# Two strips of columns for each half's 32x32 products in a block inverse, with the copies split by even and odd blocks

## The chip, the cores and the metric

The kernel runs on one core of one Trainium2 chip. The metric is the device time of one execution in microseconds (us), as the median of several runs. The engines are TensorE (PE for its matmuls, PEld for its weight loads), VectorE (DVE), ScalarE (ACT), GpSimd (POOL) and SyncE (SP, which here only issues DMAs). Each has its own queue of instructions and works through it in order; an instruction that waits for another engine waits on a semaphore and holds up what is queued behind it.

## The reference, cut to what matters

The reference is one decoder layer on 512 tokens of width 1024: a norm, one combined input projection, two mixers side by side (native sparse attention and RWKV-7), gates that merge them, an output projection, and a gated MLP with a short convolution. The change lies in the RWKV-7 mixer, whose recurrence over tokens reads:

```python
    def step(state, inp):
        r_t, w_t, k_t, v_t, a_t, b_t = inp
        sa = jnp.einsum('bhij,bhj->bhi', state, a_t)
        state = state * w_t[:, :, None, :] + sa[..., None] * b_t[:, :, None, :] + v_t[..., None] * k_t[:, :, None, :]
        return state, jnp.einsum('bhij,bhj->bhi', state, r_t)
```

There are 8 heads of size 64. The kernel cuts the 512 tokens into 8 chunks of 64 and works a chunk at a time with matrices. Within a chunk, the term `sa` of a token depends on those of the tokens before it, through a strictly triangular 64x64 matrix N. The kernel needs the inverse of I - N, for each chunk and head: 64 matrices in all.

## The kernel before, in words

A 64x64 triangular inverse is put together from 32x32 blocks. With T1 and T2 the inverses of the two diagonal blocks and N21 the block off the diagonal, the remaining block of the inverse is T2 N21 T1. The 64 matrices lie in the tile `AB`, on 128 partitions. Index `g` (0 or 1) names two groups of 32 matrices each: group 0 uses partitions 0 to 63, group 1 partitions 64 to 127. Index `b` names the first or second half of a group's partitions, so `half(g, b)` is a set of 32 partitions: 0 to 31, 32 to 63, 64 to 95 or 96 to 127. `q` counts the 32 matrices ("blocks") of a group.

The steps around the change, in the order of the code:

- Lines 618 to 633: VectorE computes all 128 inverses of the diagonal blocks at once, in the tile `inv`, row by row.
- Lines 729 to 735: VectorE transposes them, two instructions into `Y1` (line 730) and four into `AB` (line 735). `Y1` is a view of the second and third of the four columns of the tile `sg1`.
- `below(q0)`, line 740: for 16 blocks from `q0` on, and for both groups, one 32x32 by 32x32 product N21 T1. Then ScalarE copies the results from PSUM into `Y1`, through the helper of line 123.
- `left(q0)`, line 749: the second product, which multiplies by T2, and ScalarE's copy of the results into `AB`.
- Lines 760 to 774: TensorE's order is written out by hand here: one dense projection, `below(0)`, `below(16)`, and then parts of another projection (`kv_proj(1, 280)`) in turns with `left(0)` and `left(16)`. VectorE and ScalarE are ordered by a scheduler.
- From line 930 on: the sequential part over chunks. Its first pieces on TensorE are `x_own(0)` (line 922), more parts of the projection, and `compress()` (line 786), which compresses keys and values for attention. `compress()` first makes VectorE add position rows into `Rk` (lines 787 to 796), which again is the memory of `sg1`, the part under `Y1` included; its products (line 808) read `Rk` and weights `raw` that SP has loaded.

A float32 matmul appears in the trace as two passes, each with a weight load and a matmul record. The 32x32 products name two places in TensorE's array: the partitions that the operands come from choose a strip of rows, and the partitions of PSUM that the result goes to choose a strip of columns. All products of one group and one function use one strip of rows and one strip of columns: for `below`, group 0 has rows 0 to 31 and columns 32 to 63, group 1 rows 64 to 95 and columns 96 to 127. PSUM is used through `pa()` and `pb()`, two banks each in turn (`ps_a` and `ps_b`, lines 113 to 117); group 0 writes an `a` bank, group 1 a `b` bank.

The names in the profile: `sg` as an input of a 32x32 product is `Y1`; `ps_a<-sg,AB` and `ps_b<-sg,AB` are `below`, `ps_a<-AB,sg` and `ps_b<-AB,sg` are `left`. `sg<-ps_a` and `sg<-ps_b` (32x512) are ScalarE's copies of `below`, `AB<-ps_a` and `AB<-ps_b` those of `left`. `ps_b<-UV,AB` at 180.30 us is `x_own(0)`. `sg<-QK,prm` are the additions into `Rk`, `ps_mm<-raw,sg` the products with it. `ps_mm<-whi,hh`, `<-whi,hl` and `<-wlo,hh` with 280 columns are the projection that runs between the steps. `whi` and `wlo` are the two parts into which a loaded weight `raw` is split, by ScalarE and by VectorE or GpSimd.

Of the kernel before, what the change touches and what calls it, by code (L numbers as in the profile page):

```python
# [80 lines left out]
def hybrid_block(ctx: ExitStack, tc: tile.TileContext, A: dict, out: bass.AP):  # L81
# [28 lines left out]
    def mmb():  # L110
        return bank("mm", 4)

    def pa():
        return bank("a", 2)

    def pb():
        return bank("b", 2)

    def mm(o, l, r, start, stop):
        te.matmul(o, lhsT=l, rhs=r, start=start, stop=stop)  # L120

    def act(o, i, f=AF.Copy, **kw):
        sc.activation(o, i, f, **kw)  # L123
# [493 lines left out]
    ABq = [AB.rearrange("p c a r t -> p (c a) r t")[:, :, g, :] for g in range(2)]  # L617
# [110 lines left out]
    Y1 = sg1[:, 1:3].rearrange("p m s -> p (m s)").rearrange("p (q s) -> p q s", q=32)  # L728
# [8 lines left out]
    def half(g, b):  # L737
        return slice(64 * g + 32 * b, 64 * g + 32 * b + 32)

    def below(q0):  # L740
        ptr = [pa(), pb()]
        for i in range(16):
            for g in range(2):
                mm(ptr[g][half(g, 1), 32 * i:32 * i + 32], ABq[g][half(g, 0), q0 + i, 32:64], Y1[half(g, 0), q0 + i],
                   True, True)
        for g in range(2):
            act(Y1[half(g, 1), q0:q0 + 16].rearrange("p q s -> p (q s)"), ptr[g][half(g, 1)])

    def left(q0):
        ptr = [pa(), pb()]  # L750
        for i in range(16):
            for g in range(2):
                mm(ptr[g][half(g, 0), 32 * i:32 * i + 32], Y1[half(g, 1), q0 + i], ABq[g][half(g, 1), q0 + i, 32:64],
                   True, True)
        for g in range(2):
            act(ABq[g][half(g, 0), q0:q0 + 16, 32:64], ptr[g][half(g, 0)].rearrange("p (q t) -> p q t", t=32))

    fill = kv_proj(1, 280)
    urgent.clear()
    with tc.manual_schedule(engines={mybir.EngineType.PE, mybir.EngineType.Pool}):  # L760
        for m in range(NGA):
            act(siga[m], dense_fm(hh, hl))
        below(0)
        below(16)
        next(fill)
        left(0)
        next(fill)
        left(16)
        next(fill)
        norm_keys(0)  # L770
        rstd(qss.rearrange("p t h -> p (t h)"), DH)
        for t in range(NT):
            nc.gpsimd.tensor_tensor(heads(qn[:, t]), heads(qn[:, t]), qss[:, t, :, None].to_broadcast([128, 8, DH]),
                                    op=ALU.mult)
# [515 lines left out]
    with tc.manual_schedule(engines=KTS):  # L1290
        for t in range(NT):
            qs = slice(128 * t, 128 * t + 128)
            p = mmb()
# [88 lines left out]
```

## Time and profile before

| | |
|---|---|
| median of 3 runs | 843.86 us (843.79 to 844.13) |
| the profiled execution's own time | 844.05 us |
| its span on the core | 842.3 us |
| PE busy | 829.1 us, 98% of the span |
| DVE, ACT, POOL busy | 514.0, 405.9, 52.4 us |
| granted TensorE clock | 1.0 |
| the 256 records of 32x32 products | 168.74 to 178.23 us |

Times in the trace count from the start of the span. A row of the timeline gives the start of a run of equal instructions, the time it covers, the engine, the line, the operation, the output and inputs, the shape and the number of instructions; an idle time before it and its releaser stand in brackets. "32\*32" before a matmul's shape is the number of rows and columns of the array in use. Matmuls are pipelined: the duration of a record is much longer than the distance to the next start, so distances of starts tell the rate. The timeline gives two decimals, so a rate is best read over many starts.

### The profile page before, as it was taken

To read this page: it belongs to the slowest core of one execution; us is meant where nothing else is said; L and a number is where in the kernel's file an instruction comes from. 1 tells how busy PE (TensorE), PEld (TensorE's weight loads), DVE (VectorE), ACT (ScalarE), POOL (GpSimd) and SP (SyncE) were. 2 spreads that over 40 slices of the span, in tenths; PEclk is the share of its full clock that TensorE was granted. 3 is DMA by queue.
4 is the path that set the end of the run, shared out by engine and by line. 5 is a ranking of instruction groups with operands and counts; after the bars stand their busy time and mean duration, and the time that the engine had idled before them with its cause. 6 is when DMAs were issued, how large, how long until landed. Compare 5 with 4: busy or idle time off the path is not lost.

```text
span 842.3 us, 12845 instructions
## 1 busy us (share of the span) xinstructions
PE 829.1 (98%) x5097; PEld 674.3 (80%) x5097; DVE 514.0 (61%) x998; ACT 405.9 (48%) x784; POOL 52.4 (6%) x69
## 2 busy tenths in 40 slices
PE   7999999999999999999999999999999999999998
PEld 6777778887787886777788988888888888888886
DVE  5477779963556678888675576666556666322222
ACT  6766655452545677677344454444444444221210
POOL 6200020140000110111000000000000000000000
PEclk9999999999999999999999999999999999999999
DMA  7432222335461320010167033333333332223421
GB/s 228 115 82 68 75 75 76 92 104 156 126 126 51 88 63 13 22 31 26 51 204 234 0 99 90 90 97 100 100 100 100 96 90 93 98 100 113 138 75 51
DMA packets 109104, 78.73 MB, mean 93 GB/s; under 512 B 3869, under 2 KB 97748, under 8 KB 109044
## 3 DMA queue, kind: packets, MB, share of 16 engines
q1 hardware_dynamic: 106512, 73.51, 30.0%
q0 software_dynamic: 1472, 1.86, 1.0%
q10 hardware_dynamic: 1060, 2.55, 1.0%
q8 instruction: 40, 0.66, 0.3%
q14 instruction: 20, 0.16, 0.1%
HBM read 74.56 MB, written 2.29 MB: 91 GB/s over the span
## 4 chain that ended last, share of the span: by engine, by line
PE 53%; DVE 0%; DVEq 0%; issue 0%
PE ps_mm L120 52%; PE ps_b L203 0%; PE ps_a L203 0%; PE ps_a L120 0%; PE ps_b L1186 0%; PE ps_mm L1186 0%; DVE x L126 0%; DVEq L1378 0%; PE ps_a L1138 0%
## 5 line engine op out<-in xcount | busy, mean ns | idle before, releaser
L296 DVE TENSOR_TENSOR wlo<-raw,whi 128x1024 fp32r<-128x1024 f32 (+1 forms) x111 | 131.5, 1186 | 187.2 <-PE ps_mm L120 158.8
L120 PE MATMUL ps_mm<-hh,whi 128*128 128x512 f32 (+1 forms) x624 | 242.6, 391 | 0.0
L120 PE MATMUL ps_mm<-hl,whi 128*128 128x512 f32 (+1 forms) x624 | 240.4, 387 | 0.0
L123 ACT ACTIVATE whi<-raw 128x1024 fp32r<-128x1024 f32 (+3 forms) x124 | 123.3, 996 | 171.1 <-PE ps_mm L120 143.0
L120 PE MATMUL ps_mm<-hh,wlo 128*128 128x512 f32 (+1 forms) x624 | 151.8, 384 | 0.0
L120 PEld LDWEIGHTS ps_mm<-hh,whi 128*128 128x128 f32 x624 | 117.3, 188 | 26.7 <-issue 1.3
L120 PEld LDWEIGHTS ps_mm<-hl,whi 128*128 128x128 f32 x624 | 117.4, 188 | 23.5 <-issue 1.0
L120 PEld LDWEIGHTS ps_mm<-hh,wlo 128*128 128x128 f32 x624 | 115.1, 188 | 23.4
L120 PE MATMUL ps_mm<-whi,aT 128*128 128x512 f32 x352 | 84.5, 390 | 0.0
L120 PEld LDWEIGHTS ps_mm<-whi,aT 128*128 128x128 f32 x352 | 65.9, 188 | 14.3 <-issue 0.4
L135 DVE SCALAR_TENSOR_TENSOR cgv<-ps_mm,cw,cgv 128x511 f32<-128x511 f32 (+1 forms) x88 | 65.4, 746 | 1.6
L123 ACT ACTIVATE cgv<-ps_mm,cw 128x512 f32<-128x512 f32 x44 | 34.3, 781 | 23.3 <-PE ps_mm L120 23.3
L120 PE MATMUL ps_mm<-wlo,aT 128*128 128x512 f32 x176 | 44.3, 389 | 0.0
L123 ACT ACTIVATE P<-P,nm 128x512 f32<-128x512 f32 (+3 forms) x64 | 35.4, 553 | 14.9 <-DVE nm L1160 14.9
L123 ACT ACTIVATE aT<-cgv 128x512 fp32r<-128x512 f32 x22 | 13.9, 632 | 56.8 <-DVE cgv L126 56.8
L120 PEld LDWEIGHTS ps_mm<-wlo,aT 128*128 128x128 f32 x176 | 33.0, 188 | 6.9
L123 ACT ACTIVATE cgv<-cgv 128x512 f32<-128x512 f32 x22 | 13.9, 632 | 41.0 <-DVE cgv L135 41.0
L296 POOL TENSOR_TENSOR wlo<-raw,whi 128x512 fp32r<-128x512 f32 (+3 forms) x13 | 20.4, 1569 | 203.9 <-PE ps_mm L120 148.1
L1160 DVE CUSTOM_DVE_ANT_0 P<-ps_a,AB 128x512 f32<-128x512 f32 (+3 forms) x64 | 29.4, 484 | 4.2 <-PE ps_a L120 3.7
L126 DVE TENSOR_TENSOR x<-x,ps_mm 128x512 f32<-128x512 f32 (+1 forms) x17 | 11.0, 654 | 22.6 <-PE ps_mm L120 20.2
L126 DVE TENSOR_TENSOR aT<-cgv,aT 128x512 fp32r<-128x512 f32 x22 | 15.2, 693 | 14.7 <-ACT aT L123 14.7
L120 PE MATMUL ps_a<-KH,qst 128*128 128x512 f32 (+3 forms) x64 | 21.3, 348 | 1.5 <-DVE nm L1160 0.9
(356 smaller groups left out, 1201.7 us busy)
## 6 DMA issues: line engine op xcount, KB each, us to landing
raw<-in_w_up_dram SPq DMA_DIRECT2D x44, 512.0 KB, 3.8
raw<-in_w_in_dram SPq DMA_DIRECT2D x38, 512.0 KB, 3.9
raw<-in_w_down_dram SPq DMA_DIRECT2D x22, 512.0 KB, 3.6
raw<-in_w_out_dram SPq DMA_DIRECT2D x8, 512.0 KB, 3.9
xt<-in_x_dram SPq DMA_DIRECT2D x4, 512.0 KB, 5.8
raw<-in_cmp_w_k_dram SPq DMA_DIRECT2D x4, 512.0 KB, 4.4
raw<-in_cmp_w_v_dram SPq DMA_DIRECT2D x4, 512.0 KB, 4.4
raw<-in_w_proj_b_dram SPq DMA_DIRECT2D x8, 256.0 KB, 2.7
```

Of the source, the lines that this page charges most:

```text
L120: te.matmul(o, lhsT=l, rhs=r, start=start, stop=stop)
L123: sc.activation(o, i, f, **kw)
L126: v.tensor_tensor(o, a, b, op=op)
L135: v.scalar_tensor_tensor(o, a, s, b, op0=op0, op1=op1)
L296: eng.tensor_tensor(lo, raw, hi.bitcast(F32), op=ALU.subtract)
L1160: v.tensor_tensor_reduce(out=P[:, i], in0=sp[:, N * (i - i0):N * (i - i0) + N], in1=BT[:, h, 384 - 128 * qt:512], scale=-1.0, scalar=-NEG, ...
```

## The change

Within `below` and `left`, block `i` of a group used one strip of columns. Now even `i` use the strip that all of them used before, and odd `i` use the strip of the group's other half: the result goes to `half(g, 1 - i % 2)` in `below` and to `half(g, i % 2)` in `left`. Two neighbouring blocks take the same columns of the bank (offset `o`), on different partitions, so that each strip fills 256 columns of its bank instead of 512. The copies are split accordingly: for each group one copy of the even blocks and one of the odd blocks, each of 32 partitions and 256 columns, read from two different sets of partitions and written to every second block of the same destination. Products, operands and results are the same in number and size: 128 products, and 16 copies in place of 8.

In the program as built, the instructions of all engines stand in the same order as before; ScalarE has a pair of 32x8x32 copies where it had one of 512 columns. Three groups of matmuls have one more wait, on TensorE's own semaphore: the first of `left(0)`, the first of `left(16)` and the first of `x_own(0)`, since each reuses a bank whose last writers were other strips of rows.

```diff
     def below(q0):
         ptr = [pa(), pb()]
         for i in range(16):
             for g in range(2):
-                mm(ptr[g][half(g, 1), 32 * i:32 * i + 32], ABq[g][half(g, 0), q0 + i, 32:64], Y1[half(g, 0), q0 + i],
+                o = 32 * (i // 2)
+                mm(ptr[g][half(g, 1 - i % 2), o:o + 32], ABq[g][half(g, 0), q0 + i, 32:64], Y1[half(g, 0), q0 + i],
                    True, True)
         for g in range(2):
-            act(Y1[half(g, 1), q0:q0 + 16].rearrange("p q s -> p (q s)"), ptr[g][half(g, 1)])
+            for e in range(2):
+                act(Y1[half(g, 1), q0 + e:q0 + 16:2],
+                    ptr[g][half(g, 1 - e), 0:256].rearrange("p (q s) -> p q s", s=32))
 
     def left(q0):
         ptr = [pa(), pb()]
         for i in range(16):
             for g in range(2):
-                mm(ptr[g][half(g, 0), 32 * i:32 * i + 32], Y1[half(g, 1), q0 + i], ABq[g][half(g, 1), q0 + i, 32:64],
+                o = 32 * (i // 2)
+                mm(ptr[g][half(g, i % 2), o:o + 32], Y1[half(g, 1), q0 + i], ABq[g][half(g, 1), q0 + i, 32:64],
                    True, True)
         for g in range(2):
-            act(ABq[g][half(g, 0), q0:q0 + 16, 32:64], ptr[g][half(g, 0)].rearrange("p (q t) -> p q t", t=32))
+            for e in range(2):
+                act(ABq[g][half(g, 0), q0 + e:q0 + 16:2, 32:64],
+                    ptr[g][half(g, e), 0:256].rearrange("p (q t) -> p q t", t=32))
```

## The prediction

> **What bounds the kernel now.** I read the page first, for the engine that carries the span, then the busy time of the three places that the change touches, then TensorE's timeline inside them.
>
> ```profile
> span 842.3 us, 12845 instructions
> PE 829.1 (98%) x5097; PEld 674.3 (80%) x5097; DVE 514.0 (61%) x998; ACT 405.9 (48%) x784; POOL 52.4 (6%) x69
> ...
> PE 53%; DVE 0%; DVEq 0%; issue 0%
> ```
>
> TensorE is busy for 98% of the span, and the chain that ended last is all TensorE as far back as it goes. Time taken out of TensorE's queue shortens the kernel, unless something that TensorE needs comes too late for the earlier place.
>
> ```profile
> core 0: us, PE busy (x), PEclk, DMA share, GB/s
> 168.74:170.88 2.14, 2.14 (x129) 1.00 0.03 8
> 174.17:175.30 1.13, 1.13 (x65) 1.00 0.01 3
> 177.03:178.16 1.13, 1.13 (x65) 1.00 0.00 0
> ```
>
> These three stretches are both calls of `below`, then `left(0)` and `left(16)`: 4.40 us together (one record in each belongs to the next product), with no wait in them and the clock at full speed. All that the change can win on TensorE is in here. What paces them is seen in the starts:
>
> ```profile
> 168.74 0.21 PE L120 MATMUL ps_a<-sg,AB 32*32 32x32 f32 x1
> 168.75 0.21 PE L120 MATMUL ps_b<-sg,AB 32*32 32x32 f32 x1
> 168.79 0.19 PE L120 MATMUL ps_a<-sg,AB 32*32 32x32 f32 x1
> 168.80 0.19 PE L120 MATMUL ps_b<-sg,AB 32*32 32x32 f32 x1
> 168.82 0.19 PE L120 MATMUL ps_a<-sg,AB 32*32 32x32 f32 x1
> ...
> 170.75 0.19 PE L120 MATMUL ps_a<-sg,AB 32*32 32x32 f32 x1
> 170.76 0.19 PE L120 MATMUL ps_b<-sg,AB 32*32 32x32 f32 x1
> 170.88 0.40 PE L120 MATMUL ps_mm<-whi,hh 128*128 128x280 f32 x1
> ```
>
> Each group has 64 passes here. From its second start (168.79) to its 64th (170.75) lie 62 steps in 1.96 us: 31.6 ns for a pass in one place of the array. The second group starts 0.01 us behind the first and then both wait for the rest of the 31.6 ns. So the two places are each full, and the queue that feeds them is not: it can hand over the next pass within 0.01 us.
>
> **The change part by part: the matmuls.** The question is whether two strips of columns under the same strip of rows run side by side. The old code never does that with 32x32 products, but other lines share all their rows:
>
> ```profile
> 180.30 0.68 PE L120 MATMUL ps_b<-UV,AB 64*64 64x64 f32 x16
> ...
> 190.11 0.69 PE L120 MATMUL ps_a<-UV,BKT 128*64 128x64 f32 x16
> 190.62 0.64 PE L120 MATMUL ps_a<-UV,AB 128*64 128x64 f32 x16
> ...
> 238.46 0.92 PE L120 MATMUL ps_mm<-QK 128*32 128x64 f32 x24
> ```
>
> The first row alternates two 64x64 places with different rows and different columns; the next one two halves of the columns under all 128 rows. Both move 64 columns for 16 passes, in 0.68 and 0.69 us. Sharing the rows costs 0.01 us in 16 passes, so I take two strips under one set of rows as independent. The last row is 24 passes on four strips of 32 columns under all rows, 12 of them on the first; in 0.92 us they cannot have run one behind another at the 0.51 us that 8 passes of this width take in one place (190.11 to 190.62): that would be 1.5 us.
>
> So `below(0)` and `below(16)` go from 64 passes in each of two places to 32 in each of four: 32 x 31.6 ns = 1.01 us less. Each `left` goes from 32 to 16: 0.51 us less, twice. The fourth place starts some 0.01 us later than the second did, in each of three stretches: 0.03 us back. The sum on TensorE is 1.01 + 2 x 0.51 - 0.03 = 2.0 us. From both sides: nothing, if the places took turns; at most 2.2 us, half of the 4.40 us, which would need the start and the change of tiling to halve too. I take 2.0, since the rows that share their strips are that near to those that don't.
>
> [...]
>
> **The copies.** ScalarE had four copies of 32x512 in a row, now eight of 32x256.
>
> ```profile
> 124.01 1.53 ACT L123 ACTIVATE QK<-ps_mm 64x256 f32<-64x256 f32 x4
> ...
> 170.13 0.59 ACT L123 ACTIVATE sg<-ps_a 32x512 f32<-32x512 f32 x1
> 170.74 0.59 ACT L123 ACTIVATE sg<-ps_b 32x512 f32<-32x512 f32 x1
> ...
> 174.33 0.67 ACT L123 ACTIVATE whi<-raw 128x560 fp32r<-128x560 f32 x1 [1.77 <-issue]
> ...
> 178.87 0.59 ACT L123 ACTIVATE AB<-ps_b 32x512 f32<-32x512 f32 x1
> 180.40 0.28 ACT L123 ACTIVATE QK<-ps_mm 128x128 f32<-128x128 f32 x1 [0.94 <-PE ps_mm L120]
> ```
>
> The nearest row for 256 columns out of PSUM is four in 1.53 us, about 0.39 each; old ones follow each other at 0.61. Eight take 3.1 us where four took 2.4; the bounds are 2.4 (no fixed cost) and 4.9 (nothing saved by halving). `below`'s copies start at 170.13 behind other work of ScalarE, and now end at 173.2. Those that `left(0)` reads, the first four, are ready at 171.7; it starts at 174.17 - 1.0 = 173.2. `left(0)`'s copies follow the `whi` split, which itself follows TensorE, and end near 175.6; `left(16)`'s end near 177.8, against `x_own(0)` at 180.30 - 2.0 = 178.3. The cover is 1.5 us at the first place and 0.5 at the second, so I cost the copies at nothing. At 0.61 each the first four would still be ready by 172.6, and the four that `x_own(0)` needs by 178.2.
>
> **The waits.** `left(0)`, `left(16)` and `x_own(0)` also wait for TensorE's own earlier products, whose records ended over 0.5 us before: nothing.
>
> **What comes too late for the earlier place.** VectorE does not move along. It transposes and then norms without a pause:
>
> ```profile
> 167.53 7.97 DVE L735 STREAM_TRANSPOSE AB<-inv 32x1024 f32<-32x1024 f32 x4
> ...
> 175.94 0.17 DVE L126 TENSOR_TENSOR rs_y<-kss 128x8 f32<-128x8 f32 x1
> ...
> 177.28 1.36 DVE L126 TENSOR_TENSOR rs_y<-kss 128x8 f32<-128x8 f32 x1
> ...
> 179.11 1.27 DVE L126 TENSOR_TENSOR sg<-QK,prm 128x248 f32<-128x248 f32 x2
> 179.75 0.09 DVE L790 MEMSET sg<- 128x32 f32 x1
> 180.30 1.28 DVE L126 TENSOR_TENSOR sg<-QK,prm 128x248 f32<-128x248 f32 x2
> 180.94 0.09 DVE L790 MEMSET sg<- 128x32 f32 x1
> ```
> ```profile
> 168.94 1.97 POOL L296 TENSOR_TENSOR wlo<-raw,whi 128x840 fp32r<-128x840 f32 x1 [3.83 <-PE ps_mm L120]
> ...
> 177.24 1.37 POOL L296 TENSOR_TENSOR wlo<-raw,whi 128x560 fp32r<-128x560 f32 x1 [6.33 <-ACT AB L123]
> ...
> 182.31 0.81 PE L120 MATMUL ps_mm<-wlo,hh 128*128 128x280 f32 x5
> 183.05 1.95 PE L120 MATMUL ps_mm<-raw,sg 128*64 128x256 f32 x16
> 184.93 0.40 PE L120 MATMUL ps_mm<-whi,hh 128*128 128x280 f32 x1
> ```
>
> The second transpose into `AB`, which `left(0)` needs, is through at 167.53 + 7.97/2 = 171.5, before 173.2. But the additions into `Rk` end at 180.30 + 1.28 = 181.58, and the products `raw,sg` read them. Those run at 183.05 now, directly behind the projection, with 1.47 us of slack. They would come at 183.05 - 2.0 = 181.05, so 0.5 us before the additions end. The first product (keys) reads the part that was added long before; the second (values) needs the last addition, and TensorE's queue waits there in order, with the rest of the projection and the whole kernel behind it. With 0.06 us allowed for the handing over, an estimate, it goes on at 181.64, 1.41 us earlier than before.
>
> Can these additions come earlier? They wait in VectorE's order, not for TensorE. A tiny addition took 1.36 us at 177.28, where an equal one took 0.17 at 175.94; it ended as the GpSimd split of 177.24 did (178.61), so it sat that split out. The split starts when TensorE has let go of the other `wlo`, that is 1.5 us earlier now, near 175.74. VectorE is then at the start of the same chain and will sit it out there: it saves at most 0.2 us (the two instructions that come before 175.94 might pass). So the additions end between 181.4 and 181.6, and TensorE gains 1.4 to 1.6 us here. I take 1.45.
>
> After this place every step follows TensorE: the next weight, for example, is loaded when `raw,sg` is through.
>
> ```profile
> 185.48 0.46 SPq L267 DMA_DIRECT2D raw<-in_w_in_dram  x1
> ...
> 190.62 1.06 ACT L123 ACTIVATE whi<-raw 128x1024 fp32r<-128x1024 f32 x1 [1.99 <-DMA raw<-in_w_in_dram]
> ...
> 192.92 0.50 PE L120 MATMUL ps_mm<-hh,whi 128*128 128x512 f32 x1
> ```
>
> Its load and split move along; even if they did not, the split would end at 191.68, only 0.2 us after the product's new place, 192.92 - 1.45 = 191.47. The sum: 844.05 - 1.45 = 842.60 for the profiled execution, which lies 0.19 us above the median of the runs; on the median's scale 843.86 - 1.45 = 842.4.
>
> **The rivals.** *The full 2.0 us come through*, 841.9 us: if the additions end 0.5 us earlier. For it: 1.2 of VectorE's time in this chain is the sitting out, and it would vanish if the split fell beside the last transposes, which ran beside the split of 168.94 undisturbed. Against it: that needs the split 0.3 us earlier than I get, before 175.4.
>
> *The places take turns, or the queue is what paces them*: no gain, 843.9. Two places start a pass every 15.8 ns on average; if that were the rate of the queue, four would only share it. Against it: the 0.01 us between the groups' starts.
>
> *Slower: weights can't load beside the other strip.* If a load had to wait until the same rows are idle, each pass would cost what the first one does, 168.74 to 168.79, some 0.05 us instead of 0.0316, in each of two row strips. There are 128 passes in each: 128 x 0.021 = 2.7 us more, 846.5. It decides from 45 ns a pass on (1.69 us over 128). [...] The rows at 190.11 speak against it.
>
> **How the numbers follow.** I take 0.2% (1.69 us, that is below 842.17 or above 845.55) as what a measurement here can tell from no change. My forecast gets 0.52, by its own spread 842.1 to 842.6; with runs that spread by 0.3 us, 0.10 of it falls below 842.17. The full gain gets 0.20, no gain (or part of it lost later) 0.16, slower 0.12. Faster: 0.10 + 0.20 = 0.30. Within: 0.42 + 0.16 = 0.58. Slower: 0.12. The range reaches from the full gain with 0.2 of spread, 841.7, to no gain, 843.9; it leaves out the slower case.
>
> **What the profile after would show.** Four places: `ps_a` starting twice in 32 ns, both `below` in 1.13 us instead of 2.14, each `left` in 0.63. Sixteen copies of 0.36 to 0.39 us that nobody waits for. A wait of TensorE on VectorE at the first `raw,sg`, of 0.5 us or so, and `raw,sg` ending near 183.5. Wrong would be: stretches of unchanged length (taking turns), a wait at `left` or `x_own` on ScalarE, no wait at `raw,sg`, or an end that moved by another amount than `raw,sg` did.

## The result, and the profile after

The changed kernel takes 842.54 us (median of 22 runs, 842.31 to 843.26) against 843.86 us of the kernel before (22 runs, 843.65 to 844.22). The ratio is 0.9984, with a 95% interval of 0.9978 to 0.9991: 1.3 us faster, and inside the 0.2% that the prediction called no change. The forecast was 842.4 us. The profiled execution took 842.31 us, the lowest of the 22, so its distance to the profiled execution of before (1.74 us) is larger than that of the medians (1.32 us); a part of the text below is about why.

Its span is 840.5 us. First the busy times and the three stretches of TensorE, from the page and from the stretches of the changed kernel (columns as in the prediction):

```profile
PE 827.2 (98%) x5097; PEld 672.2 (80%) x5097; DVE 514.2 (61%) x998; ACT 407.1 (48%) x792; POOL 52.4 (6%) x69
```
```profile
core 0: us, PE busy (x), PEclk, DMA share, GB/s
168.71:169.98 1.27, 1.27 (x129) 1.00 0.00 0
173.26:173.95 0.69, 0.69 (x65) 1.00 1.04 370
175.68:176.37 0.69, 0.69 (x66) 1.00 0.00 0
```

The stretches fell from 2.14, 1.13 and 1.13 us to 1.27, 0.69 and 0.69 us: 4.40 to 2.65, or 1.75 us less. The starts on TensorE's timeline show four places:

```profile
168.71 0.21 PE L120 MATMUL ps_a<-sg,AB 32*32 32x32 f32 x1
168.72 0.21 PE L120 MATMUL ps_b<-sg,AB 32*32 32x32 f32 x1
168.73 0.21 PE L120 MATMUL ps_a<-sg,AB 32*32 32x32 f32 x1
168.73 0.21 PE L120 MATMUL ps_b<-sg,AB 32*32 32x32 f32 x1
168.77 0.19 PE L120 MATMUL ps_a<-sg,AB 32*32 32x32 f32 x1
```

`ps_a` and `ps_b` start twice each before the first place comes round again, at 168.77. The copies, on ScalarE:

```profile
170.09 0.76 ACT L123 ACTIVATE sg<-ps_a 32x256 f32<-32x256 f32 x2
170.88 0.78 ACT L123 ACTIVATE sg<-ps_b 32x256 f32<-32x256 f32 x2
...
177.26 0.76 ACT L123 ACTIVATE AB<-ps_b 32x256 f32<-32x256 f32 x2
```

Two copies take 0.76 us, and the next pair starts 0.79 us after the first: 0.39 us a copy. The last copy of `left(16)` ends at 178.02 (177.26 + 0.76), and `x_own(0)` on TensorE starts at 178.50. TensorE waits for none of these copies. And the place where the prediction saw something come too late, VectorE first, then GpSimd, then TensorE:

```profile
167.52 8.12 DVE L735 STREAM_TRANSPOSE AB<-inv 32x1024 f32<-32x1024 f32 x4
...
175.96 1.37 DVE L132 TENSOR_SCALAR qss<-rs_m 128x32 int32<-128x32 int32 x1
...
179.29 1.24 DVE L126 TENSOR_TENSOR sg<-QK,prm 128x248 f32<-128x248 f32 x2
...
180.46 1.27 DVE L126 TENSOR_TENSOR sg<-QK,prm 128x248 f32<-128x248 f32 x2
```
```profile
175.89 1.41 POOL L296 TENSOR_TENSOR wlo<-raw,whi 128x560 fp32r<-128x560 f32 x1 [4.98 <-ACT AB L123]
```
```profile
181.25 2.48 PE L120 MATMUL ps_mm<-raw,sg 128*64 128x256 f32 x16
183.66 0.39 PE L120 MATMUL ps_mm<-whi,hh 128*128 128x280 f32 x1
```

The bracket of the GpSimd row names a copy of ScalarE, but that copy had ended 0.24 us before the split here, and 0.63 us before it in the kernel before. In both kernels the split starts 0.14 us after the twelve products `ps_mm<-wlo,hh` of the projection have ended (175.75 here, 177.10 before), so it most likely waited for TensorE to let go of the other `wlo`, as the prediction has it.

The additions end at 181.73 and the group `raw,sg` takes 2.48 us, where it took 1.95 before: its products for the keys start at 181.25, those for the values only behind the last addition. That is a wait of 0.53 us. The list of waits of TensorE's matmuls doesn't show it, as the group as a whole is running; the list of its weight loads has 0.3 us of it, for `sg` of VectorE. Behind it TensorE is 1.24 us ahead of before: 183.66 - 168.71 = 14.95 us after the start of `below`, against 184.93 - 168.74 = 16.19.

### The profile page after: what moved, and what is told of

It is laid out like the page before. It is cut to its first block, busy times and chain, and to the rows that moved or that the text cites. A ratio compares the mean times of both kernels' runs of the same rounds, so it can differ in the third digit from the quotient of the medians.

```text
span 840.5 us, 12858 instructions
## 1 busy us (share of the span) xinstructions
PE 827.2 (98%) x5097; PEld 672.2 (80%) x5097; DVE 514.2 (61%) x998; ACT 407.1 (48%) x792; POOL 52.4 (6%) x69
## 3 DMA queue, kind: packets, MB, share of 16 engines
q0 software_dynamic: 1472, 1.86, 1.0%
## 4 chain that ended last, share of the span: by engine, by line
PE 53%; DVE 0%; DVEq 0%; issue 0%
PE ps_mm L120 52%; PE ps_a L203 0%; PE ps_b L203 0%; PE ps_a L120 0%; PE ps_b L1193 0%; PE ps_mm L1193 0%; DVE x L126 0%; DVEq L1385 0%; PE ps_a L1145 0%
```

## The experiments

All times are medians, and the kernel before was run beside each on the same chip. It took 844.2 us (843.7 to 845.5) beside the first four kernels, 844.26 us beside the next four and 844.19 us, on another chip, beside the last two (without the change: `UV` on ScalarE, and `below` three times): somewhat more than above. The changed kernel took 842.52 us in the first of these rounds, so the change was worth 1.68 us there and not 1.32.

**The two halves of the change alone.** In the first kernel only `below` is changed, in the second only `left`. A cut of the first, against the changed kernel (the products of `left` go back in the same way):

```diff
-            act(ABq[g][half(g, 0), q0 + e:q0 + 16:2, 32:64],
-                ptr[g][half(g, e), 0:256].rearrange("p (q t) -> p q t", t=32))
+        act(ABq[g][half(g, 0), q0:q0 + 16, 32:64], ptr[g][half(g, 0)].rearrange("p (q t) -> p q t", t=32))
```

> Only below uses four places and has its copies split; left is as before. Theory (what TensorE saves passes through as long as the additions into Rk, which end at 181.6, are there before the first raw,sg): below's stretch falls from 2.14 us to the 1.27 us of the changed kernel, so TensorE is 0.9 us earlier from there on; raw,sg would start at 183.05 - 0.9 = 182.15, after the additions, without a wait. 843.86 - 0.9 = 842.95. Rival 1 (the places or the copies give nothing by themselves, the gain of the changed kernel came from left): 843.86. Rival 2 (whatever is won ahead of raw,sg is cut by a fixed share there): about two thirds of 0.9, 843.25.

> Only left uses four places; below is as before. Theory: each of the two stretches of left falls from 1.13 to 0.69 us, 0.9 us together, raw,sg comes 0.9 us earlier and finds its additions done: 843.86 - 0.9 = 842.95. The two gains of this run and of the one with below alone then add up to 1.8 us, against 1.32 us of the full change; the 0.5 us between them is the wait on VectorE at raw,sg. Rival (the two parts share nothing, and the full change is simply their sum): each about 0.66, 843.2.

Measured: `below` alone 843.27 us (842.72 to 843.95), ratio 0.9988 (0.9979 to 0.9997); `left` alone 843.49 us (842.95 to 844.18), ratio 0.9989 (0.9980 to 0.9998). On TensorE's timeline of the one, then of the other:

```profile
168.92 0.21 PE L120 MATMUL ps_a<-sg,AB 32*32 32x32 f32 x1
...
182.35 1.95 PE L120 MATMUL ps_mm<-raw,sg 128*64 128x256 f32 x16
```
```profile
168.94 0.21 PE L120 MATMUL ps_a<-sg,AB 32*32 32x32 f32 x1
...
182.34 1.95 PE L120 MATMUL ps_mm<-raw,sg 128*64 128x256 f32 x16
```

From the start of `below` to `raw,sg` it was 183.05 - 168.74 = 14.31 us before; it is 13.43 and 13.40 now. So each half is worth 0.9 us on TensorE and there is no wait in `raw,sg` (1.95 us in both): the theory holds up to there. In the times it doesn't show so plainly. `below` gained 0.93 us and `left` 0.71, and the two ratios are the same within their intervals. Together that is 1.64 us, as much as the 1.68 us of the whole change beside them, where the theory had 1.8 against 1.32. By the medians alone the rival, that the whole change is the sum of its halves, fits better. The profiles show that the halves lose time too, in another place: the whole change waits in `raw,sg`, and the halves wait later, at 219.5 us (the last pair of experiments).

**The additions ahead of the norms.** In the changed kernel VectorE's order is written out in this stretch, and the additions are made as soon as their memory is free. A cut (inside `compress()`, the additions whose memory is free first also come first):

```diff
-    with tc.manual_schedule(engines={mybir.EngineType.PE, mybir.EngineType.Pool}):
+    with tc.manual_schedule(engines={mybir.EngineType.PE, mybir.EngineType.Pool, mybir.EngineType.DVE}):
 ...
         left(16)
+        cp_ = compress()
+        next(cp_)
         next(fill)
         norm_keys(0)
```

> The changed kernel, with VectorE's order written out in this stretch: the last four additions into Rk and their two memsets stand before the norms of the keys and queries, not behind them. Theory: the additions wait only for left(16) to have read Y1 (176.4) and take 4 x 0.64 + 2 x 0.09 us, so they end near 179.1, or 1.2 us later if one sits out the GpSimd split that ends at 177.3; both are before 181.25. The wait of 0.53 us of TensorE at the first raw,sg goes, and the norms end 2.7 us later than now, for which nobody waits. 842.54 - 0.5 = 842.0. Rival 1 (the kernel gets the 0.5 us back anyway at 219.5, where before had TensorE wait 0.4 us for UV and the profile of the changed kernel did not): no change, 842.5. Rival 2 (the norms, now later, hold up Xs, UV or GpSimd): slower than 842.5 by what they hold up.

> The changed kernel itself on this chip, with a second profile. Theory: 842.5, raw,sg again waits 0.5 us for the additions, and TensorE is 1.27 us ahead of before behind raw,sg. Open: whether the 0.5 us that the first profile won back at 219.5 comes again (then the profiled time is near 842.3) or not (near 842.8).

Measured: 842.19 us (841.76 to 842.48, ratio to before 0.9974, 0.9963 to 0.9984) with the additions first, 842.52 us (842.40 to 843.41, ratio 0.9980, 0.9971 to 0.9989) for the changed kernel beside it. VectorE, GpSimd and TensorE with the additions first:

```profile
175.91 0.61 DVE L126 TENSOR_TENSOR sg<-QK,prm 128x248 f32<-128x248 f32 x1
176.42 1.70 DVE L126 TENSOR_TENSOR sg<-QK,prm 128x248 f32<-128x248 f32 x1
...
178.58 0.61 DVE L126 TENSOR_TENSOR sg<-QK,prm 128x248 f32<-128x248 f32 x1
...
181.63 0.18 DVE L132 TENSOR_SCALAR qss<-rs_m 128x32 int32<-128x32 int32 x1
```
```profile
175.96 1.75 POOL L296 TENSOR_TENSOR wlo<-raw,whi 128x560 fp32r<-128x560 f32 x1 [5.00 <-ACT AB L123]
```
```profile
181.30 1.95 PE L120 MATMUL ps_mm<-raw,sg 128*64 128x256 f32 x16
183.18 0.40 PE L120 MATMUL ps_mm<-whi,hh 128*128 128x280 f32 x1
```

The additions end at 179.19, `raw,sg` takes 1.95 us again, and TensorE is 183.18 - 168.77 = 14.41 us behind the start of `below`, 0.54 less than in the changed kernel. So the wait was VectorE's order and nothing else. The same integer instruction that took 1.37 us beside the GpSimd split takes 0.18 us away from it; it had sat the split out. Now an addition does so: three of the four take 0.61 us, and the one that starts at 176.42 takes 1.70 us, to 178.12, where the split ends at 177.71. The split itself took 1.75 instead of 1.41 us. That the additions end so near to the expected 179.1 is luck: they began 0.5 us before the 176.4 of the expectation, and one took 1.1 us longer. Of the 0.53 us the median kept 0.33. The intervals of the two ratios overlap, but the runs hardly do: the highest with the additions first is 842.48, the lowest of the changed kernel 842.40.

The second profile of the changed kernel shows the wait again: `raw,sg` took 2.50 us.

**The copies without the strips, and the strips not in turns.** In the first of these kernels each group keeps its one strip, and only the copies are split. In the second, blocks 0 to 7 of a call go to one strip and 8 to 15 to the other. Of each only the product of `below` is shown, against the changed kernel; `left` and the copies follow it:

```diff
-                o = 32 * (i // 2)
-                mm(ptr[g][half(g, 1 - i % 2), o:o + 32], ABq[g][half(g, 0), q0 + i, 32:64], Y1[half(g, 0), q0 + i],
+                o = 256 * (i % 2) + 32 * (i // 2)
+                mm(ptr[g][half(g, 1), o:o + 32], ABq[g][half(g, 0), q0 + i, 32:64], Y1[half(g, 0), q0 + i],
```
```diff
-                o = 32 * (i // 2)
-                mm(ptr[g][half(g, 1 - i % 2), o:o + 32], ABq[g][half(g, 0), q0 + i, 32:64], Y1[half(g, 0), q0 + i],
+                o = 32 * (i % 8)
+                mm(ptr[g][half(g, 1 - i // 8), o:o + 32], ABq[g][half(g, 0), q0 + i, 32:64], Y1[half(g, 0), q0 + i],
```

> The strips of columns stay as before (one for each group); only the copies are split by even and odd blocks, 16 of 32x256 in place of 8 of 32x512, out of the two halves of the bank. Theory: 0.39 us a copy, hidden behind TensorE at all three places: the three stretches take 2.14, 1.13 and 1.13 us as before, TensorE is in time with before within 0.05 us behind each, ratio to before 1.000. Rival (the copies hold up left or x_own, and the strips hide it in the changed kernel): TensorE 0.1 to 0.5 us late from 174 or 180 on.

> The changed kernel, but blocks 0 to 7 of each call on one strip of columns and blocks 8 to 15 on the other, not in turns. Theory (TensorE takes its passes in the order of the program and looks ahead only a few, so the other strip is idle while 16 passes in a row go to the first): the stretches are as long as before, 2.1 us for below and 1.1 for each left, and the time is that of before, ratio 1.000. Rival (passes wait by place and are picked from far ahead): 1.27 and 0.69 us as with turns, ratio 0.998.

Measured: the copies alone 844.03 us (843.66 to 844.46) against 844.26 us, ratio 0.9998 (0.9989 to 1.0008), nothing, as expected: `raw,sg` starts 182.99 - 168.68 = 14.31 us behind `below`, as before. The strips not in turns 843.61 us (843.37 to 844.08), ratio 0.9993 (0.9984 to 1.0003). The three stretches of the latter:

```profile
core 0: us, PE busy (x), PEclk, DMA share, GB/s
169.02:170.88 1.86, 1.86 (x129) 1.00 0.00 0
174.17:175.21 1.04, 1.04 (x66) 1.00 0.22 74
176.94:177.98 1.04, 1.04 (x66) 1.00 0.00 0
```

They are 0.28 and 2 x 0.09 us shorter than before, not equal to before, and far from 1.27 and 0.69. `below` changes its strip three times and each `left` once, so each change of strip saves 0.09 us, the time of three passes of 31.6 ns. An estimate from these two figures: passes go out in the order of the program, and some three for each strip of rows (0.09 us over 31.6 ns) wait at their place while the next ones already start elsewhere. No row of the trace shows that waiting itself, and the expectation had left it out. The gain of the change comes from the turns.

**Three times as many passes.** Here every product of `below` is made three times, with the change and without it:

```diff
-        for i in range(16):
+        for i in 3 * list(range(16)):
```

> The changed kernel with every product of below done three times into the same place: 384 passes in place of 128. Rival A (each place takes its 31.8 ns a pass, four side by side, and only the beginning is slower): 256 more passes at 7.95 ns, the stretch grows from 1.27 us by 2.04 to 3.3 us. Theory B (what comes to the places is the limit from about the 37th pass on, 9.2 ns a pass as in the rest of the stretch): it grows by 2.36 to 3.6 us. The copies behind it and left then come later; the additions do not, so the wait at raw,sg goes, and the kernel is 1.5 to 1.9 us longer than the changed one.

> The kernel before the change, with every product of below done three times: 384 passes on two places. With four places TensorE stood still for 2.4 us behind the 209th pass and for 2.1 us 128 passes later, waiting for no other engine. Theory (its instructions come in blocks of 256, that is 128 passes with their weight loads, one block in 4.0 us there): two places take 3.3 us for the first 209 passes, so the first stop is about 1.1 us, the second 2.0 us, and the stretch takes 9.1 us, as long as with four places. Rival (at 15.8 ns a pass the instructions come fast enough): no stop, 384 x 15.8 ns = 6.1 us.

Measured, one run each: 852.22 us with four places and 854.17 us with two. Both theories of the first are wrong by far: the stretch of `below` took 9.16 us instead of 3.3 or 3.6. With four places, in stretches without the stops, and at the first stop:

```profile
core 0: us, PE busy (x), PEclk, DMA share, GB/s
168.73:170.48 1.75, 1.75 (x208) 1.00 0.00 0
173.09:174.79 1.70, 1.70 (x128) 0.50 0.68 234
177.09:177.88 0.79, 0.79 (x49) 0.50 0.00 0
```
```profile
170.47 0.19 PE L120 MATMUL ps_a<-sg,AB 32*32 32x32 f32 x1
173.09 0.21 PE L120 MATMUL ps_b<-sg,AB 32*32 32x32 f32 x1 [2.42 <-issue]
```
```profile
q8 instruction: 42, 0.69, 0.3%
```

And with two places:

```profile
core 0: us, PE busy (x), PEclk, DMA share, GB/s
168.73:172.02 3.29, 3.29 (x208) 1.00 0.02 6
172.94:176.07 3.13, 3.13 (x128) 0.57 0.42 144
177.22:178.50 1.28, 1.28 (x49) 0.50 0.05 13
```
```profile
172.94 0.18 PE L120 MATMUL ps_b<-sg,AB 32*32 32x32 f32 x1 [0.73 <-issue]
```

TensorE stops behind the 207th pass (104 starts on `ps_a` and 103 on `ps_b` stand before the first stop, two fewer than the expectation of the second kernel counts) and again 128 passes later, waiting for nothing that the profile shows ("issue"), and at the same place for four places and for two. The row of a queue on the page (as many packets with two places) hints at what it waits for: 42 packets of instructions, 0.69 MB, where the kernels before and after the change have 40 and 0.66 MB. So 256 matmuls and 256 weight loads more brought two packets more: 256 instructions a packet, or 128 passes. Over the whole span it is 42 packets for 5353 matmuls and 5353 weight loads, 255 a packet, if all of them are TensorE's. It goes on at 173.09 and 177.09 with four places and at 172.94 and 177.22 with two, 4.0 and 4.3 us apart, however fast the passes were before. With four places a transfer of the size of one such packet (66 GB/s in a slice of 0.25 us, 0.016 MB) stands alone between 170.75 and 171.0, 2.1 to 2.3 us before TensorE goes on; what fills these 2 us no run here shows. The estimate from these figures is a block of 256 instructions every 4.0 to 4.3 us where it is needed at once; that the 207 passes before the first stop lived on what had come earlier is the author's reading, and no row shows it. The second kernel bears out the theory of blocks (from the last start before the first stop to the next 0.93 us, of which 0.73 idle, where 1.1 was expected) and excludes its rival. Its stretch was longer than expected, 9.91 instead of 9.1 us: the granted clock fell to 0.50 behind the stop, the next 128 passes took 3.13 us instead of 2.0, and the second stop was 1.15 us. The changed kernel's 128 passes in 1.15 us ran without such a stop.

Inside the first 1.75 us the pace can be read: the 207 passes start between 168.73 and 170.47, 8.4 ns a pass; four places of 31.6 ns could take one each 7.9 ns. No run has more than four places, so whether passes could come faster than that stays open.

**The wait of 219.5 us.** Between the profiles of the changed kernel and of before lies another difference, at the third group `UV,BKT` of TensorE. VectorE and TensorE before the change, then TensorE with it:

```profile
217.85 1.23 DVE L296 TENSOR_TENSOR wlo<-raw,whi 128x1024 fp32r<-128x1024 f32 x1 [1.08 <-ACT whi L123]
219.00 0.41 DVE L135 SCALAR_TENSOR_TENSOR QK<-QK,ps_mm 128x256 f32<-128x256 f32 x1
219.44 0.43 DVE L953 COPY UV<-ps_b 64x256 f32<-64x256 f32 x1
```
```profile
219.46 1.09 PE L120 MATMUL ps_a<-UV,BKT 128*64 128x64 f32 x15
...
221.00 0.50 PE L120 MATMUL ps_mm<-hh,whi 128*128 128x512 f32 x1
```
```profile
218.15 0.69 PE L120 MATMUL ps_a<-UV,BKT 128*64 128x64 f32 x16
...
219.24 0.50 PE L120 MATMUL ps_mm<-hh,whi 128*128 128x512 f32 x1
```

Counted from the start of `below`, TensorE is 1.28 us ahead at the start of this group (219.46 - 168.74 against 218.15 - 168.71) and 1.73 us behind it (221.00 - 168.74 against 219.24 - 168.71). The group took 0.69 us in the first chunk (190.11 in the prediction), and takes that here with the change. Without it it waits for the copy into `UV`, which VectorE makes behind a weight's split (217.85), which waits for ScalarE's part (1.08 us idle), which waits for the weight's load (ScalarE's split starts at 216.76, after 3.32 us idle). In the kernel with `left` alone, where TensorE comes 0.75 us earlier and the loads of this execution (844.18 us, the slowest of its eleven) took longer, it waits more:

```profile
218.71 0.33 PE L120 MATMUL ps_a<-UV,BKT 128*64 128x64 f32 x2
220.09 0.62 PE L120 MATMUL ps_a<-UV,BKT 128*64 128x64 f32 x13 [1.04 <-DVE UV L957]
```

The profiles side by side; the load is the first `raw<-in_w_in_dram` behind `raw,sg`, from its issue to the start of the split on ScalarE, and the wait is the time from the first to the last start of the group over the 0.46 us that it takes in other chunks:

```
kernel            load, us             group starts   wait
before            185.48 -> 190.62     219.46         0.46
below alone       184.78 -> 190.39     218.72         0.89
left alone        184.77 -> 190.96     218.71         1.37
copies alone      185.42 -> 190.72     219.36         0.71
not in turns      185.29 -> 190.49     219.27         0.35
after, again      184.03 -> 189.69     218.38         0.19
after             183.81 -> 188.96     218.15         0.00
additions first   183.73 -> 188.92     217.67         0.00
```

The loads took 5.1 to 6.2 us, and what one took more was still there 30 us later: in all eight VectorE's copy into `UV` starts 28.2 to 28.9 us behind that split on ScalarE. To test it, ScalarE makes both copies of the third chunk, before the next split, with the additions first as above; once with the change and once without it:

```diff
-            v.tensor_copy(UV[64:128, c, :, 1, :], U[64:128, 0:256].rearrange("p (a d) -> p a d", d=DH))
+            (act if c == 2 else v.tensor_copy)(UV[64:128, c, :, 1, :], U[64:128, 0:256].rearrange("p (a d) -> p a d", d=DH))
```

> The kernel with the additions first on VectorE, and in the third chunk both copies into UV on ScalarE (VectorE's stood behind a weight's split there). Theory (the spread of the runs, and the 0.5 us by which the profiles differ behind 219.5, are TensorE's wait there for this copy, which hangs on how long the weight loads from 184 us on take): the third group of UV,BKT takes 0.69 us whatever the loads do, and the median falls from 842.2 to 841.8, near the lowest run of the kernel without this step (841.76). Rival (the spread is elsewhere): 842.2 as before, with the same spread.

> The kernel before the change, with the same two steps as the last kernel: the additions into Rk ahead of the norms, and in the third chunk both copies into UV on ScalarE. Theory: the first step gives nothing here (raw,sg came 1.47 us behind the additions), the second takes away the wait at the third group of UV,BKT (0.4 us in the profile of before): 843.65. Then the change by itself, with neither of the two waits in its way, is worth 843.65 - 841.87 = 1.78 us, which is what its three stretches lost (0.88 + 2 x 0.45). Rival (the two steps are worth the same with and without the change): 844.2 - (842.5 - 841.9) = 843.6 with a wait at raw,sg gone that was never there; told apart by the profile: raw,sg takes 1.95 us before and after here, and what is gained is all at 219.5.

Measured: 841.87 us with the change (841.63 to 841.96, ratio to before 0.9971, 0.9961 to 0.9982) and 843.66 us without it (843.49 to 843.88, ratio 0.9993, 0.9984 to 1.0002). The group, with and without:

```profile
217.78 0.69 PE L120 MATMUL ps_a<-UV,BKT 128*64 128x64 f32 x16
```
```profile
219.42 0.69 PE L120 MATMUL ps_a<-UV,BKT 128*64 128x64 f32 x16
```

The wait is gone in both, `raw,sg` takes 1.95 us in both, and the runs of each lie within 0.4 us, where those of the kernels with VectorE's copy spread by 0.6 to 1.8 us. The difference between the two, 1.79 us, is what the change is worth with neither wait in its way; 1.78 was expected, and the three stretches lost 1.75. The two ran on different chips; taken against the kernel before beside each of them, the difference is 1.86 us. The first of the two is the fastest kernel of this study, 2.0 us below the first median of before. That the lengths of the loads make the spread is read from eight profiles; no load was lengthened to prove it.

## Why the prediction was right, and where not

**The strips.** That two strips of columns under the same rows run side by side was right (`below` in 1.27 us where it took 2.14); the rows at 190.11 were the right evidence. The kernel that doesn't take the strips in turns shows that it is the turns that do it. Both rivals that denied it are out: no gain, and the slower one of 0.05 us a pass (a pass takes 0.018 us in one strip of rows). The four places did not act as two: 128 passes, each with its load, start in 1.15 us on two strips of rows, 18 ns a pass in one strip of rows, where one place needs 31.6.

**The sum on TensorE.** 2.0 us was too much: 1.75 us. The term "32 x 31.6 ns = 1.01 us less" took the four places as full. Passes came at 8.4 ns over the best long stretch, as the first 207 of the tripled kernel show, and in the changed kernel 127 steps took 1.15 us, 9.0 ns each. 0.06 us of the missing 0.14 us of `below` is the difference of 8.4 to 7.9 ns; the rest lies in the middle of the stretch and stays open.

**The copies and TensorE's own waits.** They cost nothing, as forecast, at the forecast 0.39 us a copy.

**What comes too late.** The step was right in kind and place: VectorE's integer instruction sat out the GpSimd split at 175.96 (forecast near 175.74), the additions ended at 181.73 (181.4 to 181.6), and TensorE waited 0.53 us in `raw,sg` (0.5). The gain behind it was 1.24 us where 1.45 was forecast. The term that was mis-sized is VectorE's: 1.45 stands on additions that end near 181.54 (183.05 - 1.45 - 0.06), a little earlier than before, and they ended 0.15 us later than before (181.73 against 181.58). The four transposes ahead of the chain took 8.12 us instead of 7.97, and the sitting out took as long as before, 1.37 against 1.36 us. The handing over took the 0.06 us that the prediction allowed for it: the first product of the values starts between 181.78 and 181.80. That the wait itself came out at the forecast 0.5 us is luck: TensorE's sum was 0.25 us too high, and the additions came 0.2 us too late. The rival by which the full 2.0 us come through needed the split before 175.4; it started at 175.89.

**"After this place every step follows TensorE."** This step failed, by one of the prediction's own signs of being wrong: the end moved by 1.74 us in the profiles, and the end of `raw,sg` by 1.24. TensorE already waited in before, at 219.46, for a copy that hangs on the weight loads, and a row of before said so: 1.09 us for a group that takes 0.69. I followed the loads to the first product that needs their weight and no further. The loads do move along, and by more than TensorE: the first was issued 1.67 us earlier (183.81 against 185.48). By the times the queue of loads goes on when the products for the keys are through, and those had not waited for the additions; no run tests that. So a part of the 0.53 us lost at `raw,sg` came back at 219.5: 0.5 us in one profile, 0.3 us in the other. That the median, 1.32 us, came within 0.14 us of the forecast is therefore the sum of two misses, 0.2 us too much up to `raw,sg` and 0.1 to 0.5 us too little behind it. How near it came also hangs on the round: in the next one the same change was worth 1.68 us.

## What to carry to other kernels

Small products that share their rows ran side by side on two strips of columns here, when they were issued in turns: 1.27 us for `below` against 1.86 not in turns and 2.14 on one strip. Four places paid down to 8 to 9 ns a pass, and a burst of 384 passes stopped behind its 207th for 2.42 us. What was taken out ahead of a fixed date of another engine was kept only up to that date (1.75 us on TensorE, 1.24 behind the additions): search for it in the order of each engine's queue, here VectorE's, and move that too. The groups that took longer in one place of the timeline than in others (1.09 us against 0.69, 2.48 against 1.95) had a wait inside them that the list of waits of TensorE's matmuls left out; look for these before saying that all that follows moves along.

## What the runs showed of the hardware that was not expected

- A burst of short passes stopped behind the 207th and again 128 passes later (256 instructions with the weight loads), idle for 0.73 to 2.42 us, with "issue" as the only cause in the trace. 512 instructions more brought two packets more (42 against 40) on the queue of instructions; that TensorE's instructions come in blocks of 256 is an estimate from these two figures.
- The granted clock fell from 1.00 to 0.50 at such a stop: near 171.9, inside the 2.42 us without a pass, with four places, and near 173.4, 0.4 us after the end of a stop of only 0.73 us, with two (0.57 over the 3.13 us after it). The passes then took 13.3 ns with four places.
- Beside a GpSimd split an integer instruction of VectorE that takes 0.18 us elsewhere took 1.37 us, and an addition of 0.61 us took 1.70 us. The four transposes, of which the first two ran beside the split of 168.92 (1.98 us long), took 1.98 to 2.05 us each.
- Two copies of 32x256 on ScalarE in a row took 0.64 to 0.65 us a pair out of the same 32 partitions (the kernel with split copies and one strip), and 0.76 to 0.78 us a pair where they alternate between two strips of PSUM, to the same destination.

```profile
170.06 0.64 ACT L123 ACTIVATE sg<-ps_a 32x256 f32<-32x256 f32 x2
170.72 0.65 ACT L123 ACTIVATE sg<-ps_b 32x256 f32<-32x256 f32 x2
```
